# Attention inside a hybrid two-layer block: keys moved to the partitions, row maxima as a 97th contraction row, sums over keys on GpSimd

## The chip, the cores and the metric

One core of one Trainium2 chip runs the whole program: two layers of a hybrid block (attention, state-space mixer, long convolutions, MLP) on 1024 latent and 256 context tokens of 1024 features. The metric is device time in microseconds. All arithmetic is float32 in effect: most products are taken as three float32r products of split operands (h = rounded part, l = rest).

## The reference

Only the attention of each layer is touched. For each of 6 heads, with 96 query and key features and 64 value features:

```python
def block_attention(q, k, v):
    b, lq, h, e = q.shape
    scale = 1.0 / math.sqrt(e)
    qb = q.reshape(b, lq // Q_BLOCK, Q_BLOCK, h, e).transpose(1, 0, 2, 3, 4)

    def one_block(qi):
        s = jnp.einsum('bqhe,bkhe->bhqk', qi, k, preferred_element_type=jnp.float32) * scale
        p = jax.nn.softmax(s, axis=-1).astype(v.dtype)
        return jnp.einsum('bhqk,bkhv->bqhv', p, v)
    ...
# in each layer: latents attend to context and latents, and in layer 0 context to context
    att_l = block_attention(q_l, jnp.concatenate([k_c, k_l], axis=1), jnp.concatenate([v_c, v_l], axis=1))
    if not last:
        att_c = block_attention(q_c, k_c, v_c)
```

So 1024 queries meet 1280 keys in each layer and head; in layer 0 another 256 meet 256.

## The kernel before

The program runs layer 0 and layer 1 one after the other. In each, `stage_a` makes the projections, `stage_b` mixes, and then come the output projection and the MLP. Python builds the program as streams of work units; `merge` interleaves the streams in given proportions, and a scheduler then fixes one order of instructions for each engine. At run time every engine takes its own queue in that order and waits where an operand isn't there yet.

`stage_b` merges two streams. `both` holds the rest of the state-space mixer (`ssm`), the filters of the long convolutions (`filters`) and the convolutions themselves (`hyena`); the other stream is `attention`. Eight PSUM banks are shared: attention has banks 0 to 5 (its scores in 0 to 4, products with the values and the spread of 1/sum in the first half of 5), the modulation vectors of layer 0 the second half of 5, the state-space mixer bank 6 and the transforms of filters and convolutions bank 7, and both once the mixer is done.

Queries and keys lie in DRAM (`qD`, `kD`) with features on 96 partitions, split in two parts, written by `kvq_out`. `attention` goes over three head pairs j. Of a pair it loads the keys of each head (`L821`, GpSimd's DMA queue, one place per head), the values (SP) and, every two tiles, the queries (`L827`, GpSimd's queue). A unit is one tile of 128 queries with both heads of the pair, 24 units a layer:

- `att_scores`: queries stationary, keys moving, three products (`L189` to `L191` in `mm3`) for each of 512, 512 and 256 keys, queries on the partitions of the result
- `att_softmax`: the row maximum on VectorE (`L899`), the exponential with the maximum as bias and the row sum as a by-product on ScalarE (`L900`), reciprocals, and two small products (`L905`) that spread 1/sum over columns
- `att_transpose`: 20 transposes on TensorE (`L916`), so that keys come to the partitions, and their copies to SBUF, four of 512 columns on ScalarE (`L921`) and one on VectorE (`L919`)
- `att_pv`: 10 key tiles by two heads, values stationary (64 columns), 128 columns moving, in float32 (`L928`), after the scores of the next unit; then a multiplication with 1/sum and a store to `mixD`

In layer 0 each pair starts with `att_ctx` for the context queries. The streams around it use the same engines: `split` rounds on ScalarE (`L159`) and subtracts on GpSimd or VectorE (`L161`), `scores` of the mixer has `L634`, `L636`, `L642`, the convolution's `fwd` has `L1253`, `L1260`, `L1261`, `L1270`, `L1274`, and the filters' products are `L1109`. `mixD` is read by `out_proj`, the next stage.

Of the kernel before, what the change touches and what calls it, by code (L numbers as in the profile page):

```python
# [11 lines left out]
F32R = mybir.dt.float32r  # L12
# [20 lines left out]
for _k, _w in (("dtb", 12), ("alog", 12), ("gqr", 32), ("gqs", 32), ("gkr", 32), ("gks", 32)):  # L33
# [34 lines left out]
class VRing:  # L68
    """views of tiles taken in turn"""
# [9 lines left out]
class PRing:  # L79
    """PSUM banks taken in turn"""  # L80
# [9 lines left out]
class PBank:  # L90
    """two PSUM places of 128 columns, taken in turn"""
# [8 lines left out]

class Acc:
    """PSUM place of a column tile over all tokens: two banks of latents, half a bank of ctx"""
# [8 lines left out]
class K:  # L111
# [19 lines left out]
    def t(self, slot, dtype=F32):  # L131
        """a new tile in a place"""
# [22 lines left out]
    # ---- helpers  # L155
    def split(self, src, h, l, on="pool"):
        """src = h + l, h rounded to float32r"""
# [5 lines left out]
    def wload(self, src, shape):  # L163
        """the two parts of weights"""
# [6 lines left out]
    def mm3s(self, outs, lh, ll, first, last):  # L171
        """mm3 for several column blocks [(out, rh, rl)]"""
# [8 lines left out]
    def groups(t0, n):  # L181
        """blocks of at most 512 tokens of t0..t0+n, those of ctx in a group of their own"""
# [3 lines left out]
    def mm3(self, out, lh, ll, rh, rl, first, last):  # L186
        """float32 product of split operands"""
# [5 lines left out]
    def rsq(self, out, src, n, scale, eps_ap=None):  # L193
        """out = 1/sqrt(src*scale + eps), one Newton step after exp(-ln/2)"""
# [14 lines left out]
        if out is None:  # L209
            # rows 32b..32b+31 go to columns 128b.. of a block-diagonal tile  # L210
# [25 lines left out]
    # ---- setup  # L236
    def setup(self):
# [30 lines left out]
        self.kD = self.dram([96, 2, 6, T], "kD")  # L268
        self.qD = self.dram([96, 2, 6, T], "qD")
# [27 lines left out]
    # ---- adaLN vectors  # L297
    def mod_cols(self, i, ch, j, w, n, m=None):
        """column tiles 2*ch+j.. of the modulation vectors from w, [128, n, 8, 128]; m is scratch"""
# [14 lines left out]
        if n == 2 and t >= 8:  # L314
            # the scale of two column tiles whose shift is there
# [13 lines left out]
    def modulation(self, i, lo, hi, ring):  # L329
        """by half chunks, as a stream"""  # L330
# [44 lines left out]
    def dense(self, wh, wl, t0, n, order=range(8)):  # L375
        """accumulates W^T h over tokens t0..t0+n"""
# [7 lines left out]
    def dense2(self, ws, n):  # L384
        """two column tiles, the earlier tokens of both first"""
# [14 lines left out]
    def rawtile(self, p, n):  # L400
        """evacuates projection columns into a zero-padded buffer: pad, latents, pad, ctx, pad"""
# [27 lines left out]
    def in_tm(self, i, lo, hi, cqs):  # L429
        """token-major columns of up to four token tiles: cq, ckv with their gains, k's rotary part, dt; as a stream"""  # L430
# [51 lines left out]
    def in_hy(self, i):  # L482
# [3 lines left out]
        for m in range(6):  # L486
# [7 lines left out]
            def tap(dst, a, b, rev):  # L494
                """x[dst...] = finished conv at columns a..b, reversed if asked"""
# [20 lines left out]
    # ---- state-space mixer  # L516
    def ssm(self, i):
# [6 lines left out]
        # softplus  # L524
# [18 lines left out]
        # cumulative decays  # L543
# [20 lines left out]
        # what each chunk adds to the states, put where the next chunk of either direction reads it:  # L564
        # P(c) is the state before chunk c, rows 0-63 forward, 64-127 backward; chunks 8, 9 are ctx
# [39 lines left out]
        # outputs  # L605
# [5 lines left out]
        def scores(c, done):  # L611
# [26 lines left out]
            # the scores of either direction, and x with its steps  # L638
# [25 lines left out]
        def rms(p):  # L664
            """mean squares of the feature groups"""
# [65 lines left out]
    def kvq_norms(self, i, lo, hi):  # L731
        """norms of ckv, and the eps of q's head norms, that of cq included"""
# [4 lines left out]
    def kvq(self, i, tt, cq):  # L737
        """keys, values and queries of one token tile, head norms, rotary"""
# [51 lines left out]
    def kvq_out(self, i, tt, nh, u3):  # L790
        """transposition, gains, split, to DRAM"""
        nc = self.nc
        tok = slice(128 * tt, 128 * tt + 128)
        for b in range(nh // 3):
# [8 lines left out]
            nc.sync.dma_start((self.kD if b < 2 else self.qD)[:, :, 3 * (b % 2):3 * (b % 2) + 3, tok], sv)  # L803

    def attention(self, i, mods):
        """by q tiles of head pairs; a unit's PV products follow the next unit's scores"""
        nc = self.nc
        q_, e_, p_ = self.t("H2", F32R), self.t("H3"), self.t("C0")
        qr, E, PT = VRing((q_, 0), (q_, 1024)), V(e_, 0, [2, T]), V(p_, 0, [2, T])
        tiles = list(range(8)) if i else [8, *range(8)]  # L810
        left = 36 / (3 * len(tiles))
        due = 0.0
        prev = None
        for j in range(3):
            if prev:
                self.att_pv(*prev)
                prev = None
            K_ = []
            for hh in range(2):
                K_.append(V(self.t(f"H{hh}", F32R), 0, [2, T]))  # L820
                nc.gpsimd.dma_start(K_[hh][0:96], self.kD[:, :, 2 * j + hh, :])  # L821
            v = V(self.t("U1"), 0, [10, 128])
            nc.sync.dma_start(v, self.vD[:, :, 128 * j:128 * j + 128])
            for tt in tiles:
                if tt % 2 == 0:
                    q = qr([2, 2, 256])
# [915 lines left out]
```

## Time and profile before

| | us |
|---|---|
| median of 3 runs (3754.63 to 3762.41) | 3754.71 |
| span of the profiled execution | 3763.3 |
| TensorE busy in it | 3487.8 |
| VectorE, ScalarE, GpSimd busy | 1873.6, 1334.8, 1479.6 |
| `stage_b` of layer 0 with attention in it | 470 to 1040 |
| `stage_b` of layer 1 with attention in it | 2488 to 2928 |

The profile is one execution taken by the hardware profiler; its span lies 8.6 us above the median of the runs. Times in the views are counted from the start of the span. "PE" is TensorE's products, "PEld" its weight loads, "DVE" VectorE, "ACT" ScalarE, "POOL" GpSimd, "SP" the engine that issues most DMAs. An instruction's duration on TensorE runs from its start to its end, and consecutive ones overlap, so the distance between starts, as the chain of waits gives it, is what a product costs. On VectorE and GpSimd a duration counts what the instruction waits for inside the engine too. In groups, the first number after the bar is busy time, then the mean duration in ns, then idle time of the engine ahead of them and what ended it.

### The profile page before, as it was taken

What the parts mean: (1) busy time and instruction counts of PE and PEld (TensorE: products, weight loads), DVE (VectorE), ACT (ScalarE), POOL (GpSimd) and SP (SyncE); (2) the same over time, 40 slices, a digit from 0 to 9 for tenths busy, and PEclk for the clock granted to TensorE, in tenths of its full rate; (3) what the DMA queues carried; (4) which work ended last, traced back from release to release, by engine and by line L of the source; (5) the groups of instructions that cost most, each with busy time, mean ns of one, the idle gap of its engine ahead of it and who ended that gap; (6) DMA issues with size and microseconds to landing.
All of it is one profiled execution on the core that took longest, in us unless ns stands there. A gap on an engine that the chain in (4) does not pass through costs nothing.

```text
span 3763.3 us, 53343 instructions
## 1 busy us (share of the span) xinstructions
PE 3487.8 (93%) x21380; PEld 2833.3 (75%) x21380; DVE 1873.6 (50%) x2639; ACT 1334.8 (35%) x2244; POOL 1479.6 (39%) x958
## 2 busy tenths in 40 slices
PE   6899888888899999999999989987889999999999
PEld 3778667677777888888888777766778678888887
DVE  7455587677623333333332456568776333333333
ACT  4565445554433111111111146555445321111111
POOL 2333665356443222223222233466554433333332
PEclk9899989998999999999999989998999999999999
DMA  6345757555632111112111314575445311111112
GB/s 231 96 116 158 185 155 198 159 164 151 214 102 68 51 50 52 62 57 68 62 62 57 126 48 129 156 201 145 130 120 166 97 56 45 51 45 50 46 45 73
DMA packets 263053, 399.53 MB, mean 106 GB/s; under 512 B 33316, under 2 KB 173365, under 8 KB 260886
## 3 DMA queue, kind: packets, MB, share of 16 engines
q1 hardware_dynamic: 249510, 373.71, 32.1%
q0 software_dynamic: 13296, 22.42, 3.0%
q8 instruction: 168, 2.75, 0.3%
q14 instruction: 79, 0.65, 0.1%
HBM read 315.58 MB, written 80.47 MB: 105 GB/s over the span
## 4 chain that ended last, share of the span: by engine, by line
PE 60%; DVE 6%; DMA 3%; issue 2%; ACT 1%; POOL 1%; SPq 0%; POOLq 0%; DVEq 0%; ACTq 0%
PE psum L175 16%; PE psum L178 16%; PE psum L176 16%; PE psum L189 2%; PE psum L191 2%; PE psum L190 2%; PE psum L305 1%; PE psum L928 1%; PE psum L916 1%; DVE H L636 1%; DVE st L899 1%; PE psum L355 0%; DMA U<-in_wmod_dram 0%; POOL Wl L161 0%; DVE H L784 0%
## 5 line engine op out<-in xcount | busy, mean ns | idle before, releaser
L161 POOL TENSOR_TENSOR Wl<-Wr,Wh 128x1024 fp32r<-128x1024 f32 (+2 forms) x334 | 709.8, 2127 | 1433.9 <-ACT Wh L159 1410.9
L175 PE MATMUL psum<-H,Wh 128*128 128x512 f32 (+1 forms) x2112 | 792.7, 376 | 15.5 <-ACT H L159 10.2
L176 PE MATMUL psum<-H,Wh 128*128 128x512 f32 (+1 forms) x2112 | 788.5, 373 | 2.6 <-POOL H L161 2.6
L159 ACT CAST Wh<-Wr 128x1024 fp32r<-128x1024 f32 (+2 forms) x334 | 304.7, 913 | 1102.6 <-PE psum L176 796.6
L178 PE MATMUL psum<-H,Wl 128*128 128x512 f32 (+1 forms) x2112 | 679.8, 373 | 0.5 <-POOL Wl L161 0.3
L952 DVE SCALAR_TENSOR_TENSOR H<-psum,mod,H 128x1024 f32<-128x1024 f32 (+2 forms) x440 | 409.8, 955 | 502.9 <-PE psum L178 472.9
L971 DVE TENSOR_TENSOR U<-U 128x1280 f32<-128x1280 f32 (+1 forms) x64 | 189.8, 2967 | 680.7 <-ACT U L969 369.2
L175 PEld LDWEIGHTS psum<-H,Wh 128*128 128x128 f32 x2112 | 400.5, 190 | 95.0 <-ACT H L159 10.7
L175 PE MATMUL psum<-C,Wh 128*128 128x512 f32 (+1 forms) x1200 | 456.9, 381 | 0.0
L176 PEld LDWEIGHTS psum<-H,Wh 128*128 128x128 f32 x2112 | 400.3, 190 | 74.4 <-POOL H L161 4.0
L178 PEld LDWEIGHTS psum<-H,Wl 128*128 128x128 f32 x2112 | 398.4, 189 | 74.6 <-issue 4.0
L176 PE MATMUL psum<-C,Wh 128*128 128x512 f32 (+1 forms) x1200 | 446.4, 372 | 0.0
L178 PE MATMUL psum<-C,Wl 128*128 128x512 f32 (+1 forms) x1200 | 369.8, 373 | 0.0
L175 PEld LDWEIGHTS psum<-C,Wh 128*128 128x128 f32 x1200 | 225.3, 188 | 63.7 <-issue 16.9
L178 PEld LDWEIGHTS psum<-C,Wl 128*128 128x128 f32 x1200 | 225.6, 188 | 44.2
L176 PEld LDWEIGHTS psum<-C,Wh 128*128 128x128 f32 x1200 | 225.6, 188 | 41.9
L161 POOL TENSOR_TENSOR C<-U,C 128x1024 fp32r<-128x1024 f32 (+2 forms) x69 | 181.3, 2630 | 165.5 <-ACT C L159 165.5
L189 PE MATMUL psum<-H,Wh 128*128 128x256 f32 (+1 forms) x640 | 206.1, 324 | 18.7 <-ACT H L159 8.3
L190 PE MATMUL psum<-H,Wh 128*128 128x256 f32 (+1 forms) x640 | 199.9, 313 | 23.6 <-DVE H L161 20.4
L191 PE MATMUL psum<-H,Wl 128*128 128x256 f32 (+1 forms) x640 | 200.2, 315 | 0.8 <-POOL Wl L161 0.7
L899 DVE TENSOR_REDUCE st<-psum 128x1 f32<-128x1280 f32 x96 | 142.5, 1485 | 62.0 <-PE psum L191 33.8
L900 ACT ACTIVATE H<-psum,st 128x1280 f32<-128x1280 f32 x96 | 127.4, 1327 | 97.9 <-DVE st L899 97.6
(386 smaller groups left out, 5633.4 us busy)
## 6 DMA issues: line engine op xcount, KB each, us to landing
Wr<-in_wff_dram SPq DMA_DIRECT2D x128, 512.0 KB, 3.7
U<-in_wmod_dram SPq DMA_DIRECT2D x48, 512.0 KB, 3.5
Wr<-in_t_odd_dram SPq DMA_DIRECT2D x32, 512.0 KB, 4.2
C<-in_wmod_dram SPq DMA_DIRECT2D x32, 512.0 KB, 4.5
Wr<-in_wout_dram SPq DMA_DIRECT2D x32, 512.0 KB, 3.7
Wr<-in_win_dram SPq DMA_DIRECT2D x28, 512.0 KB, 4.2
H<-cumD SPq DMA_DIRECT2D x18, 768.0 KB, 4.9
kD<-H SPq DMA_DIRECT2D x40, 288.0 KB, 3.5
```

The source lines that it names most:

```text
L159: nc.scalar.copy(h, src)
L161: e.tensor_tensor(l, src, h.bitcast(F32), op=ALU.subtract)
L175: mm(out, lh, rh, start=first, stop=False)
L176: mm(out, lh, rl, start=False, stop=False)
L178: mm(out, ll, rh, start=False, stop=last)
L189: mm(out, lh, rh, start=first, stop=False)
L190: mm(out, lh, rl, start=False, stop=False)
L191: mm(out, ll, rh, start=False, stop=last)
L899: nc.vector.tensor_reduce(st[:, 1, hh:hh + 1], p, axis=AX.X, op=ALU.max, negate=True)
L900: nc.scalar.activation(E[:, hh], p, AF.Exp, bias=st[:, 1, hh:hh + 1], accum_out=st[:, 0, hh:hh + 1])
L952: self.nc.vector.scalar_tensor_tensor(x, p(a, b - a), self.mod[i][:, row, st:st + 1], x, op0=ALU.mult, op1=ALU.add)
L971: nc.vector.tensor_tensor(r, r, r, op=ALU.mult)
```

## The change

Scores are now made with keys on the partitions: for a block of 512 queries and each of 10 key tiles, keys are stationary and queries move, so that the exponentials come out as the products with the values need them. The maximum of a query can't be a bias any more. It is found ahead in a pass of its own over the rounded parts alone (`att_max`), turned into a row, and put as a 97th contraction row beside ones in the keys. Sums over keys are added up tile by tile on GpSimd, and a product with ones adds over the partitions and spreads the sums over columns; 1/sum is made by exp(-ln) and one Newton step. There are 2 blocks for a pair, 6 a layer. `att_scores`, `att_softmax`, `att_transpose` and `att_pv` go; `att_ctx` stays and comes last in a pair. Two PSUM pairs of banks (0 to 3) take maxima and scores in turn, bank 4 the products with the values; bank 5 goes to the transforms in layer 1.

```diff
-        **{f"W{t}{j}": 1024 for t in "rhl" for j in range(2)}}
+        **{f"W{t}{j}": 1024 for t in "rhl" for j in range(2)}, "A0": 1536}
...
+class PPair:
+    def __call__(self):
+        self.i += 1
+        o = 1024 * (self.i % 2)
+        return self.k.ps[:, o:o + 1024]
...
 # setup
+        self.kD = self.dram([97, 2, 6, T], "kD")
+        self.qD = self.dram([97, 2, 6, T], "qD")
+        c = self.t("H6")
+        nc.gpsimd.memset(c[0:32, 0:T], 1.0)
+        nc.gpsimd.memset(c[32:64, 0:T], 0.0)
+        for d, n, r in ((self.kD, 0, 0), (self.kD, 1, 32), (self.qD, 0, 32), (self.qD, 1, 32)):
+            nc.sync.dma_start(d[96:97, n].rearrange("o h t -> (o h) t"), c[r:r + 6, 0:T])
...
     def attention(self, i, mods):
+        qt, e_, a_ = [self.t(s, F32R) for s in ("H2", "C0")], self.t("H3"), self.t("A0")
+        self.er, self.accr, self.rec = VRing((e_, 0), (e_, 1024)), VRing((a_, 0)), (V(a_, 1024, [512]), V(e_, 2048, [512]))
+        self.pp = PPair(self)
         for j in range(3):
...
+                nc.gpsimd.dma_start(K_[hh][0:97], self.kD[:, :, 2 * j + hh, :])
+            for b in range(2):
+                qs.append(V(qt[b], 0, [2, 2, 512]))
+                nc.gpsimd.dma_start(qs[b][0:97], self.qD[:, :, 2 * j:2 * j + 2, 512 * b:512 * b + 512])
...
+            for _ in self.att_max(qs[0], K_):
+                pass
+            yield 6
+            for b in range(2):
+                mx = self.att_max(qs[1], K_) if b == 0 else iter(())
+                for _ in self.att_block(j, b, qs[b], K_, v):
+                    next(mx, None)
...
+                    yield 3
...
+    def att_max(self, q, K_):
+        for t in range(4):
+            lh = [q[0:96, 0, hh, 128 * t:128 * t + 128] for hh in range(2)]
+            for hh in range(2):
+                p = self.pp()
+                for c in (0, 512):
+                    nc.tensor.matmul(p[:, c:c + 512], lh[hh], K_[hh][0:96, 0, c:c + 512], start=True, stop=True)
+                nc.vector.tensor_reduce(st[:, 0, t, hh:hh + 1], p, axis=AX.X, op=ALU.max, negate=True)
+            p = self.pp()[:, 0:512].rearrange("p (a b) -> p a b", a=2)
+            for hh in range(2):
+                nc.tensor.matmul(p[:, hh], lh[hh], K_[hh][0:96, 0, TL:T], start=True, stop=True)
+            nc.vector.tensor_reduce(st[:, 1, t], p, axis=AX.X, op=ALU.max, negate=True)
+            yield
+        nc.vector.tensor_tensor(st[:, 2], st[:, 0], st[:, 1], op=ALU.min)
+        p = self.pp()
+        for hh in range(2):
+            for t in range(4):
+                nc.tensor.matmul(p[96:128, 512 * hh + 128 * t:512 * hh + 128 * t + 128], st[:, 2, t, hh:hh + 1].to_broadcast([128, 32]), self.ident, start=True, stop=True)
+        nc.scalar.copy(q[96:97, 0], p[96:97].rearrange("p (a b) -> p a b", a=2))
+        yield
...
+    def att_block(self, j, b, q, K_, v):
+        o, acc = self.ps[:, 2048:2560], self.accr([2, 512])
+        def use(kt, E):
+            for hh in range(2):
+                nc.tensor.matmul(o[64 * hh:64 * hh + 64], v[:, kt, 64 * hh:64 * hh + 64], E[:, hh], start=kt == 0, stop=kt == 9)
+        for kt in range(10):
+            p, ks = self.pp(), slice(128 * kt, 128 * kt + 128)
+            for hh in range(2):
+                self.mm3(p[:, 512 * hh:512 * hh + 512], K_[hh][0:97, 0, ks], K_[hh][0:97, 1, ks], q[0:97, 0, hh], q[0:97, 1, hh], True, True)
+            E = self.er([2, 512])
+            nc.scalar.activation(E, p.rearrange("p (a b) -> p a b", a=2), AF.Exp)
+            if prev:
+                nc.gpsimd.tensor_tensor(acc, prev[1] if kt == 1 else acc, E, op=ALU.add)
+                use(*prev)
+            prev = kt, E
+            yield
+        use(*prev)
+        g = self.pp()[:, 0:512]
+        for hh in range(2):
+            nc.tensor.matmul(g[64 * hh:64 * hh + 64], self.ones[:, 0:64], acc[:, hh], start=True, stop=True)
+        y, t = self.rec
+        nc.scalar.activation(y, g, AF.Ln)
+        nc.scalar.activation(y, y, AF.Exp, scale=-1.0)
+        nc.vector.tensor_tensor(t, g, y, op=ALU.mult)
+        nc.vector.scalar_tensor_tensor(y, t, -2.0, y, op0=ALU.add, op1=ALU.mult)
+        nc.vector.scalar_tensor_tensor(t, o, -1.0, y, op0=ALU.mult, op1=ALU.mult)
+        nc.sync.dma_start(self.mixD[:, j, 512 * b:512 * b + 512], t)
...
     def stage_b(self, i):
-        self.gs.banks, self.gh = (6,), PRing(self, 7)
+        self.gs.banks, self.gh = (6,), PRing(self, 7, 5) if i else PRing(self, 7)
...
-                self.gh = PRing(self, 6, 7)
+                self.gh = PRing(self, 5, 6, 7) if i else PRing(self, 6, 7)
...
-    nc = _bacc.Bacc("TRN2", target_bir_lowering=False, num_devices=1)
+    nc = _bacc.Bacc("TRN2", target_bir_lowering=False, num_devices=1, dynamic_dma_scratch_size=8192)
```

## Rows read from the trace of the kernel before

**Rows 1.** Page, busy time of each engine over the span
```profile
PE 3487.8 (93%) x21380; PEld 2833.3 (75%) x21380; DVE 1873.6 (50%) x2639; ACT 1334.8 (35%) x2244; POOL 1479.6 (39%) x958
```

**Rows 2.** Busy time by stretch; columns: PE, PEld, DVE, ACT, POOL, clock, DMA
```profile
470.00:1040.00 570.00, 490.12 (x4372) 400.87 (x4370) 409.68 (x649) 288.11 (x551) 312.04 (x235) 0.91 0.59 173
...
2488.00:2928.00 440.00, 380.56 (x3325) 318.87 (x3324) 332.39 (x476) 228.41 (x400) 248.64 (x182) 0.94 0.50 144
...
480.00:640.00 160.00, 138.20 (x1385) 111.60 (x1384) 131.01 (x251) 84.88 (x161) 103.87 (x95) 0.89 0.63 179
...
2448.00:2648.00 200.00, 167.05 (x1389) 132.70 (x1389) 153.41 (x244) 108.95 (x192) 136.15 (x127) 0.93 0.62 174
...
2528.00:2568.00 40.00, 30.22 (x268) 24.51 (x268) 39.17 (x53) 22.61 (x36) 31.38 (x24) 0.91 0.40 109
```

**Rows 3.** Single instructions in order of time; columns: start us, us, engine, line
```profile
2675.38 0.76 POOL L827 DMA_DIRECT2D H<-qD  x1 [5.44 <-PE psum L191]
...
2678.01 2.35 POOL L1261 TENSOR_TENSOR H<-C 128x1024 f32<-128x1024 f32 x1 [1.88 <-DMA C<-hypD]
...
2678.45 2.99 DVE L1260 TENSOR_TENSOR H<-C 128x1024 f32<-128x1024 f32 x1
...
2681.68 4.53 POOL L1274 TENSOR_TENSOR C<-C 128x2048 f32<-128x2048 f32 x1 [1.31 <-DVE att L929]
...
2682.34 4.41 DVE L1270 TENSOR_TENSOR H<-H 128x512 f32<-128x512 f32 x1
```

**Rows 4.** Groups of DVE in layer 1's stage_b; one line's min/median/max
```profile
L636 DVE SCALAR_TENSOR_TENSOR H<-H,H 128x128 f32<-128x128 f32 x48 | 27.2, 630 | 1.5 <-POOL H L634 1.5
...
L919 DVE COPY C<-psum 128x512 f32<-128x512 f32 x24 | 16.4, 682 | 8.1 <-PE psum L916 8.1
...
L636 DVE SCALAR_TENSOR_TENSOR H<-H,H x108: 331/343/2505, 453.1 to 2650.7; 128x128 f32<-128x128 f32 x108
...
L899 DVE TENSOR_REDUCE st<-psum x96: 1471/1490/1493, 489.5 to 2917.3; 128x1 f32<-128x1280 f32 x96
...
L1270 DVE TENSOR_TENSOR H<-H x8: 677/678/4409, 833.5 to 2799.1; 128x512 f32<-128x512 f32 x8
```

**Rows 5.** Chain that ended last, 1003 to 1040 us; columns: start us, us, what
```profile
1003.23 0.37 PE psum L905 x4
...
1003.60 2.34 PE psum L916 x20
...
1020.63 2.40 PE psum L928 x40
...
1023.70 0.23 PE psum L191
```

**Rows 6.** One line's instructions: duration in ns, min/median/max
```profile
L1109 PE MATMUL psum<-H x56: 590/594/1222, 471.6 to 2533.3; 128*128 128x512 f32 x56
...
L916 PE MATMUL psum<-ident,H x960: 270/273/477, 495.1 to 2921.7; 128*128 128x128 f32 x192
```

**Rows 7.** Groups of ACT in layer 1's stage_b
```profile
L900 ACT ACTIVATE H<-psum,st 128x1280 f32<-128x1280 f32 x48 | 63.8, 1328 | 68.5 <-DVE st L899 68.4
...
L921 ACT COPY C<-psum 128x512 f32<-128x512 f32 x96 | 52.3, 588 | 19.6 <-PE psum L916 18.5 <-DMA hypD<-C 0.9
```

**Rows 8.** Chain that ended last, layer 1's stage_b
```profile
2649.78 7.52 DMA H<-kD
```

**Rows 9.** Single instructions at the start of the program
```profile
0.88 0.53 POOL L261 MEMSET r<- 128x512 f32 x1
...
2.13 0.43 SPq L286 DMA_DIRECT2D kc<-in_kc_dram  x1
...
8.30 4.60 PE L1050 MATMUL psum<-C 33*128 33x512 f32 x6 [8.30 <-DMA C<-in_feat_dram]
```

**Rows 10.** Busy time of one stretch in layer 1, columns as in rows 2
```profile
2808.00:2848.00 40.00, 40.00 (x349) 35.71 (x349) 33.04 (x47) 23.23 (x39) 26.30 (x19) 1.00 0.49 153
```

More of the change, by code (lines that the diff above doesn't have):

```diff
@@ L98, in __call__, with __init__ @@
         return self.k.ps[:, o:o + 128]
+class PPair:
+    def __init__(self, k):
+        self.k, self.i = k, 0
+    def __call__(self):
+        self.i += 1
+        o = 1024 * (self.i % 2)
+        return self.k.ps[:, o:o + 1024]
 class Acc:
@@ L802, in kvq_out @@
             nc.vector.scalar_tensor_tensor(sv[:, 1].bitcast(F32R), src, gain, sv[:, 0], op0=ALU.mult, op1=ALU.subtract)
-            nc.sync.dma_start((self.kD if b < 2 else self.qD)[:, :, 3 * (b % 2):3 * (b % 2) + 3, tok], sv)
+            nc.sync.dma_start((self.kD if b < 2 else self.qD)[0:96, :, 3 * (b % 2):3 * (b % 2) + 3, tok], sv)
     def attention(self, i, mods):
         nc = self.nc
[L808 to L813, printed above, removed]
+        qt, e_, a_ = [self.t(s, F32R) for s in ("H2", "C0")], self.t("H3"), self.t("A0")
+        self.er, self.accr, self.rec = VRing((e_, 0), (e_, 1024)), VRing((a_, 0)), (V(a_, 1024, [512]), V(e_, 2048, [512]))
+        self.pp = PPair(self)
+        steps = 60
+        left, due = 36 / steps, 0.0
         for j in range(3):
-            if prev:
-                self.att_pv(*prev)
-                prev = None
             K_ = []
@@ L820, in attention @@
                 K_.append(V(self.t(f"H{hh}", F32R), 0, [2, T]))
-                nc.gpsimd.dma_start(K_[hh][0:96], self.kD[:, :, 2 * j + hh, :])
+                nc.gpsimd.dma_start(K_[hh][0:97], self.kD[:, :, 2 * j + hh, :])
+            qs = []
+            for b in range(2):
+                qs.append(V(qt[b], 0, [2, 2, 512]))
+                nc.gpsimd.dma_start(qs[b][0:97], self.qD[:, :, 2 * j:2 * j + 2, 512 * b:512 * b + 512])
             v = V(self.t("U1"), 0, [10, 128])
             nc.sync.dma_start(v, self.vD[:, :, 128 * j:128 * j + 128])
-            for tt in tiles:
-                if tt % 2 == 0:
-                    q = qr([2, 2, 256])
-                    nc.gpsimd.dma_start(q[0:96], self.qD[:, :, 2 * j:2 * j + 2, 128 * tt:128 * tt + 256])
-                due += left
-                if tt == 8:
-                    if prev:
-                        self.att_pv(*prev)
-                        prev = None
-                    self.att_ctx(j, q[0:96], K_, v, E, PT)
-                else:
-                    regions = self.att_scores(q[0:96, :, :, 128 * (tt % 2):128 * (tt % 2) + 128], K_)
-                    if prev:
-                        self.att_pv(*prev)
-                    att = self.att_softmax(regions, E)
-                while due >= 1:
-                    next(mods, None)
-                    due -= 1
-                if tt < 8:
-                    self.att_transpose(E, PT)
-                    prev = j, tt, regions, PT, v, att
-                yield 8 if tt < 8 else 3
@@ L846, in attention @@
-        if prev:
-            self.att_pv(*prev)
+            for _ in self.att_max(qs[0], K_):
[5 more added lines that the diff above has]
+                    next(mx, None)
+                    due += left
+                    while due >= 1:
+                        next(mods, None)
+                        due -= 1
+                    yield 3
+                for _ in mx:
+                    pass
@@ L848, in attention @@
+            if i == 0:
+                q = V(qt[0], 0, [2, 2, 256])
+                nc.gpsimd.dma_start(q[0:96], self.qD[0:96, :, 2 * j:2 * j + 2, TL:T])
+                self.att_ctx(j, q[0:96], K_, v, self.er([2, 512]), self.er([2, 512]))
+                yield 3
         for _ in mods:
             pass
+    def att_max(self, q, K_):
+        nc = self.nc
+        st = self.s([3, 4, 2], "nm", 2)
+        for t in range(4):
[17 more added lines that the diff above has]
+        yield
@@ new lines, in att_block @@
+    def att_block(self, j, b, q, K_, v):
+        nc = self.nc
+        o, acc = self.ps[:, 2048:2560], self.accr([2, 512])
+        prev = None
+        def use(kt, E):
[23 more added lines that the diff above has]
+        nc.sync.dma_start(self.mixD[:, j, 512 * b:512 * b + 512], t)
```

41 lines of the change are left out of this document (removed).

## The prediction, made before the changed kernel was run

> **What bounds the kernel now.** I read the page first, then busy time by stage, then the groups of TensorE, VectorE, ScalarE and GpSimd in the stage that changes, last single instructions there. The page has TensorE busy 93% of the span [rows 1], but that is an average over stages; the change lies in stage_b, from 470 to 1040 us (layer 0) and from 2488 to 2928 us (layer 1). There TensorE is busy 490 of 570 us and 381 of 440 us, 86% both times, at a granted clock of 0.91 and 0.94; VectorE has 410 and 332 us, GpSimd 312 and 249 us, ScalarE 288 and 228 us [rows 2]. So TensorE sets the pace, with the filters, the state-space mixer and the long convolution interleaved with attention on every engine's one queue.
>
> VectorE and GpSimd have less room than they seem to. A VectorE instruction with two SBUF inputs that starts while a GpSimd one runs does nothing until that one ends: L1261 runs on GpSimd from 2678.01 to 2680.36, and L1260, started on VectorE at 2678.45, ends at 2681.44, 1.08 us after it; L1270, 0.67 us at its fastest, takes 4.41 us beside the 4.53 us of L1274 [rows 3]. L636 takes 331 ns at best and 630 ns on average in layer 1 [rows 4]. Instructions that read PSUM don't care: the row maxima stay within 1471 and 1493 ns [rows 4]. GpSimd time is therefore time taken from VectorE's SBUF work.
>
> **The change part by part.** Counts are per layer.
>
> TensorE, removed. Each of 24 query tiles has 20 transposes (2.34 us) and the spreading of 1/sum (4 instructions, 0.37 us) [rows 5]: 24 x 2.71 = 65.0 us. The products with the values are 40 instructions a tile (a float32 product is two instructions, and the two heads run side by side on halves of the columns): 24 x 2.40 = 57.6 us [rows 5]. Together 122.6 us.
>
> TensorE, added. The score products keep their columns, and an instruction of 512 columns keeps its 0.23 us [rows 5]: nothing. Products with the values now stream 512 columns. A 128-column float32 instruction comes every 0.117 us [rows 5]; one of 512 columns lasts 594 against 273 ns in the median [rows 6], 0.32 us more, so 0.44 us each and, two instructions deep, 0.88 us for a key tile with both heads; the other end is four times the old 0.24 us, 0.96 us. 60 x 0.88 = 52.8 us. The maxima's own pass is, per block of 512 queries, 16 instructions of 512 columns and 8 of 256: 16 x 0.23 + 8 x 0.12 = 4.6 us, by 6 blocks 27.8 us. Turning the minima into a row is 8 products on the same 32 columns, 16 x 0.117 = 1.9 us, by 6 is 11.2 us; the sums' products with ones 6 x 0.88 = 5.3 us. Together 97.1 us.
>
> So TensorE saves 25.5 us a layer (21 us at the other end), and at the clocks of the two stages 28 and 27 us: 55 us for both. That is all this change can give where TensorE sets the end. It is little because the values' products, in float32, cost almost what they did, and half of what the transposes give back goes to the second pass.
>
> ScalarE: 96 exponentials of 1.33 us and 192 copies of 0.59 us go for both layers [rows 7]; 120 exponentials of 1024 columns come, estimated at 1.06 us by columns, and some 2 us a block. It loses about 50 us a layer; it was busy half of the stage, so this is worth nothing by itself. VectorE: the maxima read as many columns as before; the 24 copies of 0.68 us go [rows 4], five short instructions a block come. Nothing, below zero by at most 12 us a layer, and off the bound.
>
> GpSimd: 9 additions a block, 54 a layer, of 128x1024 float32 in SBUF. The nearest row is the same form, L1261, 2.35 us [rows 3]: 127.1 us. Six query loads fewer at 0.76 us give back 4.6 us [rows 3]. Net 122.5 us, so GpSimd needs 434.5 us in layer 0 and 371 us in layer 1.
>
> Now the stage: how large a share of it can GpSimd be busy, when its queue also waits for ScalarE's roundings and VectorE's products, and VectorE's SBUF work must fit in its gaps? It had 55% and 57% on average, 65% and 68% in the busiest longer stretches, and 78% in the busiest 40 us, when VectorE was at 98% and TensorE fell to 30 of 40 us [rows 2]. In the old times the new GpSimd work would be 76% of layer 0 and 84% of layer 1. I take 76%, near the busiest 40 us because the additions fill gaps: 434.5/0.76 = 572 us (+2) and 371/0.76 = 488 us (+48), together +50. The ends: at 85% GpSimd would need 511 and 437 us, where TensorE's 542 us in layer 0 is later: -28 and -3, -31. At 72%, +33 and +75, +108; at 68% it would be +175.
>
> The wait that comes in: E has two places, so the exponential of key tile n+2 waits for the addition of tile n; behind it on ScalarE stand the roundings of the transforms' tables (L159), and behind the scores that wait for its PSUM pair stand the transforms' products on TensorE. That is how GpSimd's queue reaches the others. At a block's end the ones products wait for the last addition and the next block's first product with the values for VectorE's last read of that bank: two more of the same kind, in the 76%.
>
> Loads: keys and queries of a head pair have one place each, so at a pair's start the maxima's pass waits for a load, and the first scores for eight maxima of 1.2 us. One such load was 7.5 us of the chain [rows 8]. Six pairs could cost (7.5 + 12) x 6 = 117 us uncovered; I take nothing, since the convolutions' products cover it, and keep it as a rival. The second bank that the transforms get in layer 1 may give a few us; I take nothing.
>
> Setup: two fills of GpSimd (0.5 us for 512 columns, so 1.3 us each for 1280, as an estimate) and four DMA issues of 0.43 us on SP stand ahead of the loads on which the first products wait at 8.3 us [rows 9]. Between 0 and 4 us; I take 2.
>
> Sum: +50 + 2 = +52. The profiled run, 3763.3 us, becomes 3815 us; the median, 3754.7 us, becomes 3807 us.
>
> **The rivals.** Faster: GpSimd packs to 85%, and TensorE sets the end. The additions are nobody's next step until two tiles later, which speaks for it; against it, in layer 1 at 437 us only 66 us of idle time would be left to GpSimd, of 191. It decides from a share of 80%, where 434.5 and 371 us together fill the old 1010. -31 to -55, so 3702 to 3726 us. Chance 0.24.
>
> No change: a share of 79 to 80.5%, within 7 us of the old time, about what a measurement can tell (0.2%). 0.12.
>
> Slower still: the pairs' starts show. Once the convolutions are done nothing covers a load and eight maxima, and the loads wait on GpSimd's queue, in front of its additions. Half of the 117 us on top of the forecast gives 3865 us. The lookahead by which attention was spread over the whole stage speaks against it. 0.13.
>
> [...] 0.04.
>
> **How the numbers follow.** The forecast, shares between 72 and 78%, has 0.47: 3807 us, by itself 3770 to 3867. Faster is 0.24 + 0.04 = 0.28, the same 0.12, slower 0.47 + 0.13 = 0.60. A range from 3705 to 3880 leaves out the clock's rival, the lowest part of the first and the upper part of the third.
>
> **What would show it.** After: transposes and their copies gone, TensorE's busy share of stage_b lower, GpSimd at 75% or more of it, VectorE's two-input SBUF instructions (L636, L1253, L161) longer on average, exponentials that wait for additions. Right on the sum for TensorE would be products with the values at 0.85 to 0.96 us a key tile. Wrong would be a stage_b of layer 1 that is shorter than 440 us, or GpSimd near 85% with its queue not waited for; then the packing was too low. Time outside stage_b should move by less than 5 us.

## The result, and the profile after

The changed kernel takes 4457.1 us (median, 4452.3 to 4461.8), the kernel before 3756.5 us beside it: a ratio of 1.186 (95% interval 1.184 to 1.188), 701 us more. The forecast was 3807 us, with 3880 us as the upper end. The sign was right, the size was not.

The page of the profiled run after the change (span 4460.0 us), busy time of each engine over the span, against [rows 1]:

```profile
PE 3546.5 (80%) x19172; PEld 2739.7 (61%) x19172; DVE 1969.6 (44%) x2591; ACT 1242.7 (28%) x1968; POOL 1817.0 (41%) x1056
```

The extra time is in stage_b. For like to stand beside like, the stretches here and below begin with attention's first load, in layer 0 and in layer 1; that is 21 and 23 us earlier than the stretches of [rows 2]. Before, then after (columns as in [rows 2]):

```profile
449.00:1040.00 591.00, 499.72 (x4424) 408.49 (x4421) 426.45 (x672) 298.13 (x567) 330.98 (x249) 0.90 0.62 177
2465.00:2928.00 463.00, 399.83 (x3428) 333.28 (x3426) 342.86 (x488) 238.63 (x418) 265.02 (x201) 0.94 0.53 150
```

```profile
458.00:1436.00 978.00, 519.52 (x3304) 355.34 (x3303) 481.85 (x650) 252.03 (x426) 495.96 (x297) 0.73 0.36 107
2849.00:3637.00 788.00, 451.98 (x2362) 303.90 (x2360) 385.61 (x468) 199.61 (x288) 436.04 (x259) 0.74 0.33 92
```

The stage went from 591 to 978 us and from 463 to 788 us, 712 us for both, where the two spans differ by 697. No engine is the bound: TensorE is busy 53% and 57%, GpSimd, which the forecast wanted at 76%, 51% and 55%. All of them wait, and the question is for what. The waits of GpSimd in layer 0's stage after (line waiting, what it waited for, us in total, times, longest):

```profile
POOL H L839 <- issue: 124.8, 3, 43.9
...
POOL H L835 <- issue: 53.4, 3, 39.2
...
POOL C L839 <- issue: 25.7, 1, 25.7
```

L835 and L839 are the loads of keys and queries. GpSimd stands 204 us in front of them, up to 44 us at a time, waiting for nothing that the trace names. And when a load is under way it takes long. The DMA part of the page, first after, then before: GpSimd's queue (packets, MB), and loads (KB of one, median us from issue to landing):

```profile
q0 software_dynamic: 113328, 23.06, 2.8%
...
H<-kD POOLq DMA_DIRECT2D x12, 970.0 KB, 47.3
...
H<-qD POOLq DMA_DIRECT2D x6, 776.0 KB, 46.5
C<-qD POOLq DMA_DIRECT2D x6, 776.0 KB, 46.9
```

```profile
q0 software_dynamic: 13296, 22.42, 3.0%
...
H<-kD POOLq DMA_DIRECT2D x12, 960.0 KB, 10.3
...
H<-qD POOLq DMA_DIRECT2D x27, 384.0 KB, 5.9
```

Ten KB more, one row of 97, and a key load lands after 47 instead of 10 us; the queue carries 3% more bytes in 8.5 times the packets. What that does to a pair's start is seen in the chain that ended last, layer 1 after (start us, us, what):

```profile
2860.18 46.32 issue
2906.52 45.34 DMA H<-qD
...
2969.97 43.19 DMA C<-qD
```

135 us of one pair's start are GpSimd standing in front of a load and then two query loads, one after the other. So the suspicion: loads of 97 partitions, not the additions, are most of the 701 us.

### The profile page after: what moved, and what is told of

The parts are those of the page before. It is cut to its first block, busy times and chain, and to the rows that moved or that the text cites. A ratio compares the mean times of both kernels' runs of the same rounds, so it can differ in the third digit from the quotient of the medians.

```text
span 4460.0 us, 48618 instructions
## 1 busy us (share of the span) xinstructions
PE 3546.5 (80%) x19172; PEld 2739.7 (61%) x19172; DVE 1969.6 (44%) x2591; ACT 1242.7 (28%) x1968; POOL 1817.0 (41%) x1056
## 3 DMA queue, kind: packets, MB, share of 16 engines
q8 instruction: 151, 2.47, 0.2%
## 5 line engine op out<-in xcount | busy, mean ns | idle before, releaser
L200 PE MATMUL psum<-H,Wh 128*128 128x256 f32 (+1 forms) x640 | 211.9, 335 | 69.9 <-ACT H L170 29.8
L873 PE MATMUL psum<-H,H 96*128 96x512 f32 x96 | 46.7, 566 | 276.5 <-DMA H<-qD 156.3
L186 PEld LDWEIGHTS psum<-C,Wh 128*128 128x128 f32 x1200 | 225.3, 188 | 63.8 <-issue 16.9
L905 POOL TENSOR_TENSOR A<-A,H 128x1024 f32<-128x1024 f32 x96 | 249.8, 2602 | 22.9 <-ACT H L903 21.0
L201 PE MATMUL psum<-H,Wh 128*128 128x256 f32 (+1 forms) x640 | 208.5, 327 | 27.6 <-DVE H L172 24.5
## 6 DMA issues: line engine op xcount, KB each, us to landing
H<-kD POOLq DMA_DIRECT2D x12, 970.0 KB, 47.3
```

The source lines that it names most:

```text
L186: mm(out, lh, rh, start=first, stop=False)
L200: mm(out, lh, rh, start=first, stop=False)
L201: mm(out, lh, rl, start=False, stop=False)
L873: nc.tensor.matmul(p[:, c:c + 512], lh[hh], K_[hh][0:96, 0, c:c + 512], start=True, stop=True)
L905: nc.gpsimd.tensor_tensor(acc, prev[1] if kt == 1 else acc, E, op=ALU.add)
```

## The experiments

Four theories. A: a load of 97 partitions is not spread over the DMA engines. B: the change also halves the descriptor space of GpSimd's DMA queue, from the default to 8192, to make room for its sums, and that holds GpSimd. P: the additions on GpSimd, on its queue and by holding VectorE. M: the second pass over the scores for the maxima, with the starts of pairs. Times are medians; the kernel before stood at 3759 to 3763 us beside them.

**Loads split into 96 rows and one.**

```diff
-nc.gpsimd.dma_start(K_[hh][0:97], self.kD[:, :, 2 * j + hh, :])
+nc.gpsimd.dma_start(K_[hh][0:96], self.kD[0:96, :, 2 * j + hh, :])
+nc.gpsimd.dma_start(K_[hh][96:97], self.kD[96:97, :, 2 * j + hh, :])
 # the query loads likewise
```

> The changed kernel with each key and query load of 97 rows given as two: rows 0 to 95, and row 96 alone. The same computation. Theory A (a load of 97 partitions is not spread over the DMA engines: in the trace after, 970 KB takes 47.3 us to land where 960 KB of 96 rows took 10.3 us): the big parts land in about 10 us again, the wait of TensorE on the loads and GpSimd's 25 to 44 us stops in front of the query loads go, stage_b of layer 0 falls from 978 to 560-660 us, and the kernel comes to what the sum of the prediction gave, 3760-3880 us. [...] Theory D (starts of pairs, whichever way the rows are loaded: the max pass stands open at each of six pairs): 3865-4100 us, with TensorE waiting at pair starts though the loads land in 10 us.

3935.1 us, 1.0464 (1.0444 to 1.0483). 4457.1 - 3935.1 = 522 of the 701 us are gone with nothing but this. The loads land early again:

```profile
H<-kD POOLq DMA_DIRECT2D x12, 960.0 KB, 10.1
...
H<-qD POOLq DMA_DIRECT2D x6, 768.0 KB, 11.6
```

Theory A has the largest part, and the time is still 55 us above what theory A was expected to give at most. It lies in the range of the expectation's theory D, the starts of pairs; D is part of M here. GpSimd no longer stands in front of a load (0.2 us in the whole run, against 296 us in the trace after). 172 us are left for P and M.

**The kernel before, with 97 rows loaded.**

```diff
-self.kD = self.dram([96, 2, 6, T], "kD")
+self.kD = self.dram([97, 2, 6, T], "kD")
-nc.gpsimd.dma_start(K_[hh][0:96], self.kD[:, :, 2 * j + hh, :])
+nc.gpsimd.dma_start(K_[hh][0:97], self.kD[:, :, 2 * j + hh, :])
 # qD and the query loads likewise; row 96 is set once and read by nobody
```

> The kernel before, with nothing changed in attention but that its key and query loads take 97 rows from arrays of 97 rows (row 96 is set once and read by nobody). Theory A: 12 key loads of 970 KB at about 47 us and 27 query loads of 388 KB at about 19 us on one engine are some 1,080 us of transfer, of which most lies in the two attention stages (570 and 440 us before): 4,050 to 4,400 us. [...]

4144.0 us, 1.1012 (1.0995 to 1.1030): 381 us, in a kernel whose attention is otherwise untouched. The DMA part of its page:

```profile
H<-kD POOLq DMA_DIRECT2D x12, 970.0 KB, 51.3
...
H<-qD POOLq DMA_DIRECT2D x27, 388.0 KB, 33.8
```

That settles that the row count alone does it, without additions, maxima or key-major scores.

**One load of 112 rows.**

```diff
-self.kD = self.dram([97, 2, 6, T], "kD")
+self.kD = self.dram([112, 2, 6, T], "kD")
-nc.gpsimd.dma_start(K_[hh][0:97], ...)
+nc.gpsimd.dma_start(K_[hh][0:112], ...)
 # qD likewise; rows 97 to 111 are filled in setup by 60 more stores of one row
```

> The changed kernel with the arrays of 112 rows in DRAM and one load of 112 partitions for each key and query load (rows 97 to 111 are filled once and read by nobody). 15% more bytes than 97 rows. Theory A in the form that the number of partitions has to be divided among the engines: loads land in 10-13 us, and the time is that of the split loads within 20 us. If instead a last row beyond 96 or the row from another store was to blame, the loads stay near 47 us or over and the time over 4400 us.

3987.0 us, 1.0600 (1.0582 to 1.0618), 52 us above the split loads, not within 20. The key loads land in 10.8 us, as theory A has it; attention's first instruction starts 46 us later, at 503.6 instead of 457.3 us, which was not allowed for. The extra stores in setup stand on SP's queue ahead of a load that the first product waits for; that product starts at 58.4 us there, at 8.8 us with split loads. More rows are faster than 97: it isn't the bytes.

**The loads by themselves.** A program with nothing but loads into one tile:

```diff
+nc.gpsimd.dma_start(rv[0:n], kD[0:n, :, h, :])   # float32 rounded to float32r, n = 96, 97, 98, 100, 106, 112, 128
+nc.gpsimd.dma_start(fv[0:n], kD[0:n, :, h, :])   # float32 as it is, n = 96, 97, 98
+nc.sync.dma_start(fv[0:n], kD[0:n, :, h, :])     # SP's queue, n = 96, 97, 98
```

> Loads alone, one after the other, no attention and no other work: [n, 2, 1280] of a DRAM array into one tile, n = 96, 97, 98, 100, 106, 112, 128 from GpSimd's queue with rounding to float32r; 96, 97, 98 from GpSimd's queue without rounding; 96, 97, 98 and a single row from SP's queue. It computes nothing of the reference; the output is zeros. [...] If any count that is not a multiple of 16 is slow, 98, 100 and 106 take 40-50 us as well. [...] If rounding on the way is what costs, 97 without rounding, or from SP's queue, lands like 96.

Landing times by size; 10 KB are one row, r is the rounded tile, f the other:

```profile
r<-kD POOLq DMA_DIRECT2D x1, 1120.0 KB, 11.4
r<-kD POOLq DMA_DIRECT2D x1, 1060.0 KB, 25.2
r<-kD POOLq DMA_DIRECT2D x1, 1000.0 KB, 10.4
r<-kD POOLq DMA_DIRECT2D x1, 980.0 KB, 7.0
f<-kD POOLq DMA_DIRECT2D x1, 980.0 KB, 10.0
...
r<-kD POOLq DMA_DIRECT2D x1, 970.0 KB, 57.8
f<-kD POOLq DMA_DIRECT2D x1, 970.0 KB, 54.5
...
r<-kD POOLq DMA_DIRECT2D x1, 960.0 KB, 11.8
```

98 rows land in 7.0 us and 100 in 10.4, 112 and 128 in 11.4 and 11.7, 97 in 57.8, above the 47 us in the trace after (two such loads were under way together, at first beside the stores of the output), 106 in 25.2. SP's queue shows the same, beside GpSimd's later loads: into one tile each load waits for the last, and its issues (start us, us, line) tell how long that was for 96, 97 and 98 rows:

```profile
90.67 0.66 SPq L37 DMA_DIRECT2D f<-kD  x1
99.77 0.77 SPq L38 DMA_DIRECT2D f<-kD  x1
149.53 0.87 SPq L39 DMA_DIRECT2D f<-kD  x1
156.44 0.57 SPq L40 DMA_DIRECT2D f<-kD  x1
```

9.1, 49.8 and 6.9 us. So neither rounding nor GpSimd's queue nor a count that is not a multiple of 16 is to blame: 98 and 100 are fast. Nor are small packets: SP's queue carried 3401 packets in all, and its load of 97 rows is as slow. How many of the 16 DMA engines work can be read where only the two loads of 97 rows are under way (the last two columns are the mean busy share of the 16 engines and GB/s):

```profile
44.00:70.00 26.00, 0.00 (x0) 0.00 (x0) 1.00 0.14 53
```

0.14 of 16 is 2.2 engines for two loads, about one for each, an estimate from that share. The GB/s of the page by slices of 4 us agree: 51 to 54 in that stretch, 27 and 28 where hardly anything but SP's load of 97 rows moves (144 to 152 us), and 78 to 81 where it moves beside the load of 106 rows (104 to 120 us), so some 52 for 106, twice as much, an estimate. Of the seven counts the two slow ones are 97, which no number from 2 to 16 divides, and 106, which of these only 2 divides; the others can be divided by 10 (100), by 14 (98) or by 16 (96, 112 and 128). The landing times go with that for the counts tried; what lies behind it no run shows.

**The halved descriptor space**, in the kernel before: with loads of 97 rows, and with its own of 96.

```diff
-nc = _bacc.Bacc("TRN2", target_bir_lowering=False, num_devices=1)
+nc = _bacc.Bacc("TRN2", target_bir_lowering=False, num_devices=1, dynamic_dma_scratch_size=8192)
```

> The kernel before with loads of 97 rows (4144 us) and with the descriptor space of GpSimd's queue halved to 8192, as the changed kernel has it. Theory A: the 97 rows are what is slow, on one engine, and the halved space adds little: 4130 to 4170 us. Theory B (the halved space is what holds GpSimd in front of its next load, 25 to 44 us a time in the trace after): 30 stops more or longer ones, over 4250 us.

> The kernel before with the descriptor space of GpSimd's queue halved to 8192 and nothing else changed (loads of 96 rows). If the halved space costs only with loads of 97 rows (4144 against 4258 us), this is the time before: within 8 us of 3760. If it costs by itself, 3800 us or over, and part of what the kernel with split loads still has over the kernel before is the halved space and not the additions and maxima.

With 97 rows 4258.2 us, 114 us above the same loads with the full space; with 96 rows 3762.7 us, 0.9998 (0.9987 to 1.0009). GpSimd's waits in front of a query load, over the whole span, with 97 rows and the full space, then with half of it:

```profile
POOL H L832 <- issue: 76.5, 2, 38.7
```

```profile
POOL H L832 <- issue: 369.7, 12, 48.3
```

Two stops become twelve. So theory B is right, but only on top of A: halving the space costs nothing while loads are spread (13,296 packets in the whole run), and 114 us in that kernel when each load leaves in many small packets (205,488 in the whole run) and stays under way for 32 us (queries) or 49 us (keys, medians). Of the 522 us in the changed kernel, how much is the stop and how much the landing was not separated: no run has the changed kernel's loads of 97 rows with the full space.

**What the other 172 us are.** All on the split loads. First the additions on VectorE:

```diff
-nc.gpsimd.tensor_tensor(acc, prev[1] if kt == 1 else acc, E, op=ALU.add)
+nc.vector.tensor_tensor(acc, prev[1] if kt == 1 else acc, E, op=ALU.add)
```

> Base is the changed kernel with split loads (3935 us, 172 us above before; the 122 us that the prediction's +50 does not cover are what is to be found). The 54 additions a layer run on VectorE in place of GpSimd; the same computation. Theory P (GpSimd's additions: 135 us a layer on its queue, and VectorE held while they run): GpSimd loses 270 us, VectorE gains some 60 us a layer but loses the holding, 3830 to 3900 us. Theory M (the second pass over the scores for the maxima: 45 us of TensorE and 75 us of VectorE a layer, and the starts of pairs): VectorE has the more to do, 3930 to 3990 us.

Then the additions left out, the maxima left out, and both:

```diff
-nc.gpsimd.tensor_tensor(acc, prev[1] if kt == 1 else acc, E, op=ALU.add)   # left out; acc is set to 1 once a layer
...
-for _ in self.att_max(qs[0], K_): pass                                     # maxima left out
-mx = self.att_max(qs[1], K_) if b == 0 else iter(())
+mx = iter(())
-nc.scalar.activation(E, p..., AF.Exp)
+nc.scalar.activation(E, p..., AF.Exp, scale=0.01)
```

> Base is the changed kernel with split loads. The additions over keys are left out: the ones product reads a tile that is set to 1 once a layer. Theory P: 172 us go, but for the rest of some 30 us: 3750 to 3800 us. Theory M: 3890 to 3930 us. Shares of both show as a value between.

> Base is the changed kernel with split loads. The pass for the maxima is left out (its products, reductions, turning and copy); row 96 of q stays zero, and the exponential takes 0.01 of the scores so that nothing overflows. The additions stay. Theory M: 3750 to 3800 us, TensorE about 57 us a layer less, VectorE 75 us less. Theory P: the same GpSimd work stands in the stage, 3880 to 3930 us.

> Base is the changed kernel with split loads, without the additions and without the pass for the maxima (both as in the two kernels before it). If P and M together are what is left, and add: TensorE has some 55 us a layer less than in the kernel before, and the time falls to 3640 to 3720 us. If the layout itself (head pairs with all loads at once, blocks of 512 queries, fewer steps to interleave with the transforms) is to blame, it stays over 3760 us.

| kernel (split loads) | us | ratio to before (95%) |
|---|---|---|
| as changed | 3935.1 | 1.0464 (1.0444 to 1.0483) |
| additions on VectorE | 3841.7 | 1.0203 (1.0187 to 1.0220) |
| without additions | 3804.1 | 1.0105 (1.0089 to 1.0121) |
| without maxima | 3894.6 | 1.0344 (1.0322 to 1.0365) |
| without both | 3759.3 | 1.0001 (0.9986 to 1.0015) |

The additions are 131 us, whether taken away first (3935.1 to 3804.1) or after the maxima (3894.6 to 3759.3: 135 us); the maxima are 40 to 45 us. Theory P has three quarters of the rest, M one quarter, and they add. That the two together come out at the time before, and not 40 to 120 us below it, was not expected; it is at the edge of the case that the layout itself gives nothing. Stage_b as changed with split loads, without additions, and without both (layer 0, layer 1):

```profile
457.00:1135.00 678.00, 507.83 (x3294) 344.50 (x3292) 480.68 (x649) 250.56 (x425) 459.62 (x309) 0.85 0.53 153
2560.00:3110.00 550.00, 420.09 (x2339) 286.02 (x2338) 376.31 (x465) 197.43 (x283) 401.07 (x263) 0.85 0.46 129
```

```profile
458.00:1070.00 612.00, 489.42 (x3297) 336.45 (x3295) 430.24 (x648) 248.53 (x426) 328.02 (x256) 0.87 0.57 166
2494.00:2985.00 491.00, 417.70 (x2380) 282.84 (x2379) 332.53 (x469) 201.38 (x290) 281.38 (x218) 0.88 0.52 148
```

```profile
455.00:1040.00 585.00, 448.40 (x3053) 305.88 (x3051) 354.60 (x570) 242.41 (x418) 333.12 (x256) 0.85 0.59 171
2473.00:2922.00 449.00, 355.05 (x2093) 240.04 (x2091) 270.91 (x387) 187.31 (x277) 274.07 (x214) 0.87 0.53 150
```

The 172 us are here: 678 and 550 us, 87 more than before in each layer. Without both, TensorE works 51 and 45 us less than before, VectorE 72 us less in each, and the stages are only 6 and 14 us shorter, the whole run not at all. Attention's products with the values end at 819 us there, the convolutions' last ones at 1037 us. What TensorE waits for in layer 0's stage without both:

```profile
PE psum L200 <- ACT H L170: 16.2, 5, 13.3
PE psum L322 <- DMA C<-in_wmod_dram: 13.8, 6, 4.3
PE psum L200 <- DVE U L1276: 12.8, 13, 3.0
PE psum L201 <- DVE H L172: 12.0, 6, 7.1
PE psum L202 <- POOL Wl L172: 10.7, 13, 2.1
```

L322 are the modulation vectors, which wait for their weights. The others are the transforms' products, which wait for roundings on ScalarE, for the subtractions behind them on VectorE and GpSimd, and for VectorE's reading of their bank. Where they do so is seen when the stage of layer 0 is cut at the end of attention's products, 832 us with those of the context:

```profile
455.00:832.00 377.00, 328.84 (x2376) 202.54 (x2374) 220.62 (x422) 182.19 (x320) 190.61 (x176) 0.91 0.68 187
832.00:1040.00 208.00, 119.56 (x683) 103.34 (x679) 133.97 (x149) 60.22 (x99) 142.51 (x81) 0.75 0.44 142
```

Beside attention TensorE is busy 87% of the time, much as before (85%); after it the convolutions run 208 us alone, at 57% and a granted clock of 0.75 (layer 1: 87%, then 116 us at 57% and 0.75). So what was saved came back as an uncovered end. That says less than that the layout gives nothing: attention spread over the whole stage was not tried in this kernel, and whether it would then end earlier is open.

The additions act in two ways, and both are in the trace with split loads. The exponentials wait for them (layer 0's stage):

```profile
ACT H L905 <- POOL A L907: 32.0, 15, 4.5
```

And VectorE is held: it has 50 and 44 us more to do than without additions (481 to 430, 376 to 333), though none of the additions is its own. The line of the prediction's L636, two SBUF inputs, in layer 1, first with the additions on GpSimd, then without them (630 ns before, [rows 4]):

```profile
L653 DVE SCALAR_TENSOR_TENSOR H<-H,H 128x128 f32<-128x128 f32 x48 | 37.8, 848 | 2.3 <-POOL H L651 2.3
```

```profile
L653 DVE SCALAR_TENSOR_TENSOR H<-H,H 128x128 f32<-128x128 f32 x48 | 22.6, 533 | 2.2 <-POOL H L651 2.2
```

In layer 0 the same line hardly moves, 591 against 537 ns. On VectorE itself an addition takes 1.36 us, against 2.47 us on GpSimd, and GpSimd is busy only 14 and 6 us longer than without additions: 93 of the 131 us come back. How the 131 divide between queue and held VectorE this doesn't tell, since that edit moves both.

**A version without additions.** The product with the values can give the sums as well, if its stationary has 64 columns of ones beside a head's 64 of values:

```diff
-nc.tensor.matmul(o[64 * hh:64 * hh + 64], v[:, kt, 64 * hh:64 * hh + 64], E[:, hh], start=kt == 0, stop=kt == 9)
+nc.tensor.matmul(o, v[hh][:, kt], E, start=kt == 0, stop=kt == 9)   # v[0] is [values | ones], v[1] [ones | values]
 # heads one after the other, exponentials of 512 columns, sums taken from the other 64 partitions
```

> The same computation without any additions over keys: the stationary of a head's product with the values is 128 columns wide, 64 of values and 64 of ones, so that the sums over keys come out of the same instruction (on the other 64 partitions); loads split as before; the heads of a pair come one after the other, exponentials of 512 columns. If what is left in the kernel without additions (3804 us) is the price of the maxima and of what the stage waits for, this lands there: 3780 to 3830 us (120 exponentials of 0.6 us a layer in place of 60 of 1.0 us, 6 evacuations more). If a product with 128 stationary columns took longer than one with 64 it would show on TensorE and be 3850 us or over. If float32 products with 64 columns side by side run together for the two heads, and those with 128 can't, TensorE needs up to 65 us a layer more: 3870 to 3930 us.

3826.5 us, 1.0176 (1.0149 to 1.0203). The time is within the range for the first case, 22 us above that without additions; it is the fastest full version of the new layout, and 1.8% slower than the kernel before. For TensorE the sums are not free, though. A single product of 128 stationary columns is no longer than one of 64 (590 and 592 ns at the shortest), but the two heads' products of 64 columns ran side by side, and those of 128 did not. Layer 0, without additions, then with ones columns:

```profile
L899 PE MATMUL psum<-H,U 128*64 128x512 f32 x240 | 70.0, 639 | 2.6 <-ACT H L906 2.6
```

```profile
L903 PE MATMUL psum<-H,U 128*128 128x512 f32 x120 | 62.0, 606 | 0.5 <-ACT H L920 0.5
L903 PE MATMUL psum<-H,A 128*128 128x512 f32 x120 | 58.4, 601 | 2.1 <-DVE H L906 1.3 <-ACT H L920 0.8
```

Busy times of overlapping products overstate this. By the distance between starts, at the full clock, a key tile of both heads with its scores takes 2.59 us with split loads (648.32 to 650.91) and 3.22 us here (603.26 to 606.48): some 38 us a layer, an estimate from 60 key tiles. That is the mechanism of the third case, and yet the time is that of the first: TensorE's busy time in the stages is only 18 and 3 us above that without additions. The order of issue was tried from there:

```diff
-for _ in merge((both(), 400), (self.attention(i, mods), 120)):
+for _ in merge((both(), 400), (self.attention(i, mods), 100)):   # and 150
```

> The same as the kernel before it, but attention is issued at 100 in place of 120 parts against the 400 of mixer and convolutions. In the kernel without additions and maxima, attention was through at 820 us and the convolutions at 1038 us, with TensorE at 448 of 585 us; if the order of issue is what leaves TensorE idle there, the slower pace gives 10 to 40 us back; if the convolutions' own chain of roundings sets the end, it moves by less than 8 us; if attention now ends last, it is slower by 10 us or more.

> The kernel with ones columns with attention issued at 150 parts against 400 (it stands at 120; at 100 the time went from 3826 to 3857 us, since attention ended last). If the order of issue is still too slow for attention, it gives 10 to 30 us back: 3796 to 3816 us. If at 120 attention and convolutions end together already, 150 leaves convolutions over at the end and costs as 100 did: 3830 to 3860 us.

3857.3 us at 100 parts and 3838.9 us at 150, against 3826.5 at 120. There is no gain in it, and at 150 the intervals overlap (1.0191 to 1.0228, against 1.0149 to 1.0203). At 120 attention's last products with the values end at 962 us in layer 0, the convolutions' last ones at 1065; in layer 1 at 2975 and 2961. At 100 the latter pair is 3004 and 2977, at 150 it is 2985 and 2971, so 150 parts did not end attention earlier.

## Why the prediction was wrong

**The loads: the term that failed.** Of the loads at a pair's start the prediction said "I take nothing, since the convolutions' products cover it"; it priced one load by the 7.5 us of [rows 8], and as a rival had 117 us for six pairs, half of it taken. The row was of a load of 96 partitions; the change makes it 97, and that it would be the same load was assumed, not asked. It is 47 us in the median, and GpSimd's queue stops in front of the next one for up to 46 us. With the split loads against without, this term is 522 us. The rival's place was right, its price, 58 us, was a ninth. "Six query loads fewer at 0.76 us give back 4.6 us" failed for the same reason: the issue of a load of 97 rows by itself takes 2.90 us in the program with loads alone, where one of 96 takes 0.77 us. A sentence on it would have been due, since the diff says 0:97 in two lines. So 522 of the 701 us come from a term that stood at nothing; the direction that was forecast holds without it too.

**GpSimd's share: the right mechanism, mis-sized.** With the loads mended, the sum can be read: +50 us forecast, +172 us measured. Of these, 131 us are the additions and 40 to 45 us the maxima, which the sum had only as TensorE time that sets no end. Additions are 118.5 and 16.9 us in layer 0, 135.4 us where 127.1 were counted:

```profile
L907 POOL TENSOR_TENSOR A<-A,H 128x1024 f32<-128x1024 f32 x48 | 118.5, 2468 | 8.3 <-ACT H L905 7.8 <-ACT rqy L216 0.2
...
L907 POOL TENSOR_TENSOR A<-H 128x1024 f32<-128x1024 f32 x6 | 16.9, 2818 | 16.5 <-ACT H L905 16.4
```

GpSimd is busy 459.6 of 678 us and 401.1 of 550 us, 68% and 73%, where 76% was taken, near the 78% of the busiest 40 us of [rows 2]. The prediction's own list has "at 68% it would be +175"; the range ended at 72%. (At the other end the forecast's 3770 us is 3779 us by its own share of 78%.) The additions filled the gaps in part: in layer 0 GpSimd's waits for ScalarE's roundings fell from 130 to 64 us, but 24 us of waits for exponentials came in, and its idle time is 218 us against 260. That the rest is waits that each engine passes on to the next is read from the traces, not tested by itself. That exponentials would wait for additions, and that VectorE's two-input instructions would take longer, was right, as shown above, and so was, nearly, a key tile's price of 0.85 to 0.96 us for the products with the values: by the distance between starts it is 0.94 to 1.01 us with split loads where the clock is full (644.03 to 645.90 us for two key tiles, 648.32 to 649.33 for one).

**TensorE: the gain did not show.** 25.5 us a layer were to be saved. The pass for the maxima was counted at 39.0 us (27.8 and 11.2); taking it out, with the additions already gone, takes 41.0 us of TensorE in layer 0 and 62.6 in layer 1. The products with the values, counted at 52.8 against 57.6 us, are 72.8 us busy with split loads, 70.5 us before, at a granted clock of 0.85 against 0.91:

```profile
L898 PE MATMUL psum<-H,U 128*64 128x512 f32 x240 | 72.8, 692 | 7.9 <-ACT H L905 7.7 <-DVE H L921 0.2
```

So with the loads mended TensorE is busy 8 and 20 us more in the stage than before, not 25 us less, and with neither new part 51 and 45 us less, where the terms give 64.5. More than that, the reading "TensorE sets the pace" is in doubt: without additions and maxima TensorE has less to do and nothing ends earlier. The end there is the convolutions' chain over three other engines, with nothing beside it. Whether TensorE would set the pace if attention covered that chain to its end stays open.

**The rivals.** Faster by a packing of 85%: the share came out at 68% and 73%. The clock, at 0.04: that it would rise with the transposes of attention gone, no run here shows. Without them the granted clock of the stages is 0.73 and 0.74 after, where TensorE is busy 53% and 57%, and 0.83 to 0.89 (layer 0) and 0.84 to 0.90 (layer 1) in the runs with mended loads, below the 0.90 and 0.94 before. The kernel before with loads of 97 rows has all its transposes and fits in between: 0.79 at 63% busy (450 to 1200 us) and 0.82 at 69% (2600 to 3200 us). The starts of pairs were the case that happened, at a price nobody put on it.

**Setup** was forecast at 2 us. The first product starts 0.5 us later (8.83 against 8.30 us); attention's first load is issued at 457.3 us with split loads, at 449.2 us before.

## What to carry to other kernels

Look at the partition count of every load that a change touches: one row more than 96 made a load almost five times as long (47.3 against 10.3 us), and splitting the odd row off brought 522 us back. Price a moved or widened transfer as a new one, not by the old row. And before counting on an engine's saved time, take its work out and see whether anything ends earlier; where it doesn't, see which stream ends last and what stands beside it.

## What the runs showed of the hardware that was not expected

- Of seven row counts two were slow, and not those with the most bytes: 97 rows took 54 to 58 us (two under way together) and 49.8 us on SP's queue (beside other loads), 106 took 25.2 us, but 98 took 7.0 us and 112 took 11.4 us. No number from 3 to 16 divides 97 or 106, one from 10 to 16 each of the other five: a pattern in the counts tried. Two loads of 97 rows kept 0.14 of the 16 DMA engines busy, at 53 GB/s.
- Issuing such a load takes GpSimd longer: 2.90 us for 97 rows, 1.84 us for 106, 0.77 us for 96, in the program with loads alone. In the kernel before with 97 rows GpSimd's queue carried 205,488 packets, against 13,296 with 96.
- Half the descriptor space cost nothing with 13,296 packets and 114 us with loads of 97 rows.
- A float32 product of 512 columns took 590 ns at the shortest with 128 stationary columns, and 592 ns with 64 of one head on half of the columns. But two heads with 64 columns each ran side by side: a key tile with its scores took 2.59 us so, and 3.22 us with 128 columns for each head.
